# Three gating rows spread over the partitions by a write to memory and a broadcast read, in place of diagonals and a matmul with ones

## The chip, the core and the metric

The kernel runs on one core of a Trainium2 chip. The metric is the device time of one execution in microseconds (us). Shorter is better.

The engines are called as in the profile: PE (matrix products; PEld is its weight load), DVE (vector), ACT (scalar and activation), POOL (GpSimd) and SP (it issues most of the transfers). Each engine works through its own instructions in a fixed order and waits at the first one whose inputs are not ready. Transfers (DMAs) run on 16 DMA engines. SP and POOL each have a queue of them.

## The reference, cut to what matters

Two layers over 512 tokens of width 1024. Each layer has a mixer and an MLP, and each of the four results is multiplied by a gating row (`g1` or `g2`) of 1024 numbers that is the same for all tokens:

```python
c_act = jax.nn.silu(c)
for i in range(DEPTH):
    mod = c_act @ ada_w[i] + ada_b[i]
    sh1, sc1, g1, sh2, sc2, g2 = jnp.split(mod, 6, axis=-1)
    h = modulate(rmsnorm(x, norm_mix_g[i]), sh1, sc1)
    y = pool_mixer(...) if i == 0 else sgu_mixer(...)
    x = x + g1[:, None, :] * y
    h = modulate(rmsnorm(x, norm_mlp_g[i]), sh2, sc2)
    x = x + g2[:, None, :] * sq_relu_mlp(h, mlp_w1[i], mlp_w2[i])
return rmsnorm(x, final_g)
```

The gating row of the first mixer is handled apart and is not touched. The change is in how the other three (layer 0 `g2`, layer 1 `g1`, layer 1 `g2`) get to the place where they are multiplied.

## The kernel before, in words

Tokens lie on the 128 partitions, in four tiles of 128 tokens (`X(t)`, 128x1024). For the products the normed activations lie transposed, features on partitions, in `hb`, as a high and a low part. Each float32 product of weights and activations is three matmuls of such parts (`mm3`, lines 176 to 178). Each weight tile is loaded as `raw` (512 KB, into the three slots of the pool `w4`, helper `raw4`, line 155), and ACT makes the high part `wh` (line 167) and DVE the low part `wl` (line 168). Each of `wh` and `wl` has five slots.

**Modulation.** A column of 128 modulation numbers is the product of 128 columns of `ada_w` and `c_act`. `ada_tile` (line 191) loads a 512 KB tile into a slot of `w4` (line 194) and DVE multiplies and sums it (line 198). Two such sums make two columns of `mods[i]` (line 183). So the 1024 numbers of a gating row stand as 8 columns of 128 partitions, `mods[i][:, c_g(n,0) : c_g(n,0)+8]`.

**Spreading.** The results are multiplied with tokens on partitions, so the row must stand on every partition: the tile `gb` (128x1024). `spread_cols` (line 209) does it: `diagonals` (line 205) makes 8 diagonal matrices `dg` on POOL (line 207), PE multiplies them with a matrix of ones, 512 columns at a time (line 216), and ACT copies the two banks to `gb` (line 217). In two of the three places `dg` takes a slot of `w4`; in the third it is `dgu` in a tile of the second MLP.

**Where `gb` is read.** `gated` (line 959) multiplies each finished piece of a result by it (line 964), adds it to `x`, takes the squares on ACT (line 969), sums them (lines 973, 975), and POOL makes the reciprocal root `rr` (line 223, called by `rms`). `normed` (line 980) scales 2 token tiles by `rr` on ACT (`xs`, line 985), PE turns them (`px`, line 992), and ACT and DVE write `hb`.

**Stages.** (1) Modulation and pool mixer of layer 0, up to about 60 us. (2) `mlp(0)`: hidden units `f` and output products `p` in turn, then the units `q`, which end with `gated`. In it the list `ex` of extra work is popped at an even pace: 8 `ada_tile` of layer 0, then the spread of layer 0's `g2`, then 24 `ada_tile` of layer 1. (3) the gating mixer of layer 1 (SGU): `w_v` products, layer norm (POOL makes `rr` again), `do_u` and `do_mix` (the spread of layer 1's `g1` is the first extra work there, after `u0`), then the product with `w_o`, whose results go through `gated`; the last 8 `ada_tile` (for layer 1's `g2`) run in it. (4) `mlp(1)`: `first1` (line 1130) loads four tiles of `w1f`, and runs them over the first 256 tokens, then over the second 256. `normed(1, 1, 1)` and `spill(1)` (a copy of `x` to memory by POOL, line 1008) stand after the third tile of the first half. Then the units `f` 4 to 7, after the last of which the spread of layer 1's `g2` stands (line 952), then units `s` and `p` up to the `q` units.

**What sets the order.** PE's instructions run in the order in which the code issues them. In the first stage that holds for DVE, ACT and SP as well. Everywhere else a planner orders the instructions of SP, ACT, DVE and POOL when the program is built: at each step it gives an engine the instruction, first in program order, whose inputs and slots it holds to be ready. So a load, or one of the diagonals, can stand far ahead of its place in the code. The lines that the steps below touch are 155, 183, 194, 205 to 217, 223, 761, 964, 992, 1008, 1022 and 1074.

Of the kernel before, what the change touches and what calls it, by code (L numbers as in the profile page):

```python
# [7 lines left out]
F32 = mybir.dt.float32  # L8
F32R = mybir.dt.float32r
AF = mybir.ActivationFunctionType  # L10
ALU = mybir.AluOpType
# [3 lines left out]
P = 128  # L15
D = 1024
S = 512
KD = D // P
# [23 lines left out]
def c_sh(n, k):  # L42
    return 24 * n + 2 * k + 1


def c_g(n, k):
    return 24 * n + 16 + k
# [31 lines left out]
def decoder_kernel(ctx: ExitStack, tc: tile.TileContext, xtok, vecs, rows, fgrow, ada0, adag, ada1, pool_w, w1s, w1, w1f, w1b, w2, w2e, w_v, w_u, w_o, wsT, lnp, bs, out):  # L79
    nc = tc.nc  # L80
    V, A, G, T = nc.vector, nc.scalar, nc.gpsimd, nc.tensor
# [3 lines left out]
    w4 = ctx.enter_context(tc.tile_pool(name="w4", bufs=3))  # L85
# [20 lines left out]
    def bank(name, pool=None):  # L106
        pool = pool or ps
        return pool.tile([P, S], F32, name=name, tag="mm" if pool is ps else "xz")
# [4 lines left out]
    ones = cp.tile([P, P], F32, name="ones")  # L113
# [3 lines left out]
    ident = cp.tile([P, P], F32, name="ident")  # L117
    G.memset(ident, 0.0)
    G.affine_select(out=ident, in_=ident, compare_op=ALU.not_equal, fill=1.0, base=0, pattern=[[-1, P]], channel_multiplier=1)
    mods = [cp.tile([P, 48], F32, name=f"mods{i}") for i in range(2)]  # L120
# [16 lines left out]
    gb = big.tile([P, D], F32, name="gb")  # L137

    def X(t):
        return x_[t // 2][:, t % 2]  # L140

    def H(k, c):

        return h_[0][:, 0, k, c], h_[0][:, 1, k, c]
# [4 lines left out]
    def mod(i, c):  # L149
        return mods[i][:, c : c + 1]  # L150
# [30 lines left out]
    def finish_mods(i, b, pm):  # L181

        V.tensor_tensor(mods[i][:, 2 * b : 2 * b + 2], pm, vec[:, V_ADAB + 48 * i + 2 * b : V_ADAB + 48 * i + 2 * b + 2], ALU.add)
        n, q = divmod(b, 12)
        if q < 8:
            g0 = (V_MIX, V_MLP)[n] + 8 * i + q
            V.scalar_tensor_tensor(scl[i][n][:, q : q + 1], mod(i, 2 * b), 1.0, vec[:, g0 : g0 + 1], ALU.add, ALU.mult)
# [3 lines left out]
    def ada_tile(i, t, src, get):  # L191

        r = get()
        nc.sync.dma_start(r, src)
        b, j = divmod(t, 2)
        if j == 0:
            pmv[i, b] = sm.tile([P, 2], F32, name="pmv", tag="pmv")
        V.scalar_tensor_tensor(r, r, 1.0, cb, ALU.mult, ALU.mult, accum_out=pmv[i, b][:, j : j + 1])  # L198
        if j == 1:
            finish_mods(i, b, pmv.pop((i, b)))  # L200
# [1 line left out]
    def get4():  # L202
        return w4.tile([P, D], F32, name="ada", tag="w4")

    def diagonals(dg, cols):
        for k in range(KD):
            G.tensor_scalar(dg[:, k], ident, cols[:, k : k + 1], None, ALU.mult)

    def spread_cols(cols, dg=None):

        if dg is None:
            dg = w4.tile([P, KD, P], F32, name="dg", tag="w4")
            diagonals(dg, cols)
        for n in range(2):
            po = bank("pb")
            T.matmul(po, ones, dg[:, 4 * n : 4 * n + 4], start=True, stop=True)  # L216
            A.activation(gb[:, S * n : S * n + S], po, AF.Copy)


    def power(v, n):  # L220
# [12 lines left out]
    with (  # L233
# [67 lines left out]
        def rms():  # L301
            v0 = sm.tile([P, NT], F32, name="rv4", tag="rv4")
            V.tensor_scalar(v0, ss, RMS_EPS, None, ALU.add)
            rt.append(power(v0, NT))
# [285 lines left out]
    def parts(o, a):  # L590

        A.activation(o[0], a, AF.Copy)
        V.tensor_tensor(o[1], a, f32(o[0]), ALU.subtract)

    def mlp(i, first, extra, last, ending):
# [3 lines left out]
        with (  # L599
# [56 lines left out]
            def a_sums(step):  # L656


                def a(r, j):
                    return h32[0][:, 4 * j : 4 * j + 4, 256 * r : 256 * r + 256]  # L660

                def operand(pool, tag):
                    t = pool.tile([P, 2, 4, 256], F32R, name="as", tag=tag)
                    return t[:, 0], t[:, 1]

                def minus(o, p, q):
                    V.tensor_tensor(o, p, q, ALU.subtract)

                first, half = slice(0, 256), slice(256, 512)
                if step == 0:  # L670
                    sums_a.update({1: H(slice(0, 4), first), 2: H(slice(4, 8), first), 4: H(slice(4, 8), half)})
                    shift(hx, LINE - GAP)
                    minus(a(1, 1), a(1, 0), a(1, 1))
                    m, o = 5, operand(hx, "hx")
                elif step == 1:
                    minus(a(1, 1), a(1, 1), a(0, 0))
                    m, o = 6, operand(big, "x0")
                elif step == 2:
                    minus(a(0, 0), a(0, 0), a(1, 0))
                    V.tensor_tensor(a(1, 1), a(1, 1), a(0, 1), ALU.add)  # L680
                    m, o = 3, operand(big, "x1")
                else:
                    m, o = 7, H(slice(0, 4), half)
                parts(o, a(0, 0) if m == 7 else a(1, 1))
                sums_a[m] = o
# [214 lines left out]

            gain = mods[i][:, c_g(1, 0) : c_g(1, 0) + KD]
            done = first(put)
            if i:
                dg = su.tile([P, KD, P], F32, name="dgu", tag="u")
                diagonals(dg, gain)
            units = [("f", (0, f)) for f in range(done, 8)]
            for c in range(3):
                if i == 0:
# [17 lines left out]
            def ahead(n):  # L926

                if i == 0:
                    return min(n + 3, len(units))
                m, s = n + 1, items(*units[n])  # L930
                while m < len(units) and m < n + 5:
                    s += items(*units[m])
                    if s > 5 and m > n + 1:
                        break
                    m += 1
                return m
# [4 lines left out]
            for n, (kind, u) in enumerate(units):  # L941
                for m in range(n, ahead(n)):
                    if m not in ready:
                        ready[m] = prep[units[m][0]](units[m][1])
                while at < len(extra) and at < due * (n + 1):
                    extra[at]()
                    at += 1
                run[kind](u, ready[n])
                if i and kind == "f":
                    a_sums(u[1] - 4)  # L950
                    if u == (0, 7):
                        spread_cols(gain, dg)
                if i and u == (3, 1, 4):
                    reload()

# [24 lines left out]
    def normed(hf, i, n):  # L980

        xs = []
        for r in range(2):
            t = w4.tile([P, D], F32, name="xs", tag="w4")
            A.activation(t, X(2 * hf + r), AF.Copy, scale=rms(2 * hf + r))
            xs.append(t)
        c = slice(256 * hf, 256 * hf + 256)
        for k in range(0, KD, 2):
            px = bank("px")
            for q in range(2):  # L990
                for r in range(2):
                    T.transpose(px[:, 256 * q + P * r : 256 * q + P * r + P], xs[r][:, P * (k + q) : P * (k + q) + P], ident)  # L992
            tt = h32[0][:, k : k + 2, c] if h32 else sm.tile([P, 2, 256], F32, name="tt", tag="tmp")
            for q in range(2):
                a, b = scl[i][n][:, k + q : k + q + 1], mod(i, c_sh(n, k + q))
                if q:
                    A.activation(tt[:, q], px[:, 256:512], AF.Identity, bias=b, scale=a)
                else:
                    V.tensor_scalar(tt[:, q], px[:, 0:256], a, b, ALU.mult, ALU.add)
            parts(H(slice(k, k + 2), c), tt)  # L1000


    h32, xd = [], []
    dram = ctx.enter_context(tc.tile_pool(name="dram", bufs=1, space=bass.MemoryType.DRAM))

    def spill(h):
        xd.append(dram.tile([P, 2, D], F32, name=f"xd{h}"))
# [2 lines left out]
    def reload():  # L1010
        for h in range(2):
            x_[h] = big.tile([P, 2, D], F32, name=f"x{h}", tag=f"x{h}")
            G.dma_start(x_[h], xd[h])
        load_fg()
# [4 lines left out]
        return SWEEP  # L1019

    ex = [lambda q=q: ada_tile(0, 40 + q, ada1[q], get4) for q in range(8)]
    ex += [lambda: spread_cols(mods[0][:, c_g(1, 0) : c_g(1, 0) + KD])]
    ex += [lambda q=q: ada_tile(1, q, ada1[8 + q], get4) for q in range(24)]
    mlp(0, first0, ex, gated, lambda: normed(0, 1, 0))


# [6 lines left out]
    with (  # L1033
# [37 lines left out]
                V.tensor_tensor(v, v, lnt[:, n].rearrange("p (a b) -> p a b", a=2), op)  # L1071

        u, gt, wu = {}, {}, {}
        ex = [lambda: spread_cols(mods[1][:, c_g(0, 0) : c_g(0, 0) + KD])]
        ex += [lambda q=q: ada_tile(1, q, ada1[8 + q], get4) for q in range(24, 40)]

        def do_u(n):
# [75 lines left out]
    def last1(t, c0, n, src, y):  # L1153
# [13 lines left out]
        else:  # L1167
# [5 lines left out]
            nc.sync.dma_start(out[t, :, 1], X(t)[:, S:D])  # L1173

    mlp(1, first1, [], last1, lambda: None)


# [77 lines left out]
```

## Time and profile before

| | |
|---|---|
| median of 3 runs | 873.24 us (872.81 to 873.34) |
| the profiled execution | 873.16 us, of which the profile's span is 871.5 us |
| PE busy | 861.0 us (99%) |
| DVE busy | 670.1 us (77%) |
| ACT busy | 451.3 us (52%) |
| POOL busy | 66.9 us (8%) |
| DMA | 161.80 MB, mean 186 GB/s |
| clock granted to PE | 0.997 |

In the rows of the timeline the columns are start and duration in us, engine, line, operation, tile written and tile read, shapes and count; in brackets stand the idle time before and what ended it. A row with "SPq" or "POOLq" is the issuing of a transfer. In a table of windows each engine has its busy us and its count of instructions, then come PE's clock, the share of time in which the 16 DMA engines were busy, and GB/s.

### The profile page before, as it was taken

Reading aid. Unit: us, or ns where it says so; the run is one execution under the profiler, and the core shown is the slowest. Engines: PE = TensorE matmul, PEld = TensorE weight load, DVE = VectorE, ACT = ScalarE, POOL = GpSimd, SP = SyncE. Lnnn points to the kernel's source line nnn. Section 1 sums busy time; section 2 is a strip of 40 time slices with the busy share of each in tenths; the row PEclk is TensorE's granted clock in tenths of the full one; section 3 lists DMA queues with packets and bytes.
Section 4 is the critical chain, followed back from the end, with each engine's and each line's share of the span. In section 5 each row is a group of like instructions: output and inputs, shape, how many; then the busy total and the mean of one; then the engine's idle time right before and its main releaser. Section 6 shows DMA issues by size and latency. Waiting matters only on the chain.

```text
span 871.5 us, 11804 instructions
## 1 busy us (share of the span) xinstructions
PE 861.0 (99%) x4580; PEld 741.6 (85%) x4580; DVE 670.1 (77%) x881; ACT 451.3 (52%) x653; POOL 66.9 (8%) x87
## 2 busy tenths in 40 slices
PE   9999999999999999999999999999999999999996
PEld 7878888788888888888878888999999998999885
DVE  6889696779869886657798866667777698679755
ACT  4285755554444445237333326666765576566521
POOL 3000003000000000000410012000101000100001
PEclk9999999999999999999999999999999999999998
DMA  9969853553554341615548525937758587677302
GB/s 350 417 229 311 274 193 137 193 193 121 181 204 169 128 162 51 215 37 205 193 155 288 185 73 222 319 87 179 171 193 178 156 225 224 136 162 261 123 24 97
DMA packets 39517, 161.80 MB, mean 186 GB/s; under 512 B 4387, under 2 KB 4515, under 8 KB 34214
## 3 DMA queue, kind: packets, MB, share of 16 engines
q1 hardware_dynamic: 35282, 137.72, 44.0%
q0 software_dynamic: 4032, 23.07, 13.0%
q8 instruction: 36, 0.59, 0.3%
q10 hardware_dynamic: 148, 0.27, 0.1%
q14 instruction: 19, 0.16, 0.1%
HBM read 156.84 MB, written 4.19 MB: 185 GB/s over the span
## 4 chain that ended last, share of the span: by engine, by line
PE 97%; ACT 2%; DVE 1%; issue 0%; POOLq 0%; POOL 0%; DVEq 0%; ACTq 0%
PE po L176 17%; PE po L178 17%; PE po L177 17%; PE pm L177 12%; PE pm L176 12%; PE pm L178 12%; PE pg L389 1%; PE pq L423 1%; PE po L1097 1%; PE po L437 1%; PE pg L288 1%; ACT sq L273 1%; PE px L992 1%; PE pb L216 1%; PE pc L288 1%; PE po L564 0%
## 5 line engine op out<-in xcount | busy, mean ns | idle before, releaser
L176 PE MATMUL po<-hb,wl 128*128 128x256 f32 (+1 forms) x624 | 209.5, 336 | 1.3 <-DVE wl L168 1.3
L178 PE MATMUL po<-hb,wh 128*128 128x256 f32 (+1 forms) x624 | 207.9, 333 | 0.0
L177 PE MATMUL po<-hb,wh 128*128 128x256 f32 (+1 forms) x624 | 207.8, 333 | 0.0
L168 DVE TENSOR_TENSOR wl<-raw,wh 128x1024 fp32r<-128x1024 f32 x107 | 130.9, 1224 | 45.6 <-ACT wh L167 45.3
L167 ACT ACTIVATE wh<-raw 128x1024 fp32r<-128x1024 f32 x107 | 112.7, 1057 | 63.1 <-PE pm L178 31.8
L176 PE MATMUL pm<-wh,ol 128*128 128x512 f32 x336 | 130.8, 389 | 0.0
L178 PE MATMUL pm<-wh,oh 128*128 128x512 f32 x336 | 130.8, 389 | 0.0
L177 PE MATMUL pm<-wl,oh 128*128 128x512 f32 x336 | 130.8, 389 | 0.0
L176 PEld LDWEIGHTS po<-hb,wl 128*128 128x128 f32 x624 | 117.2, 188 | 14.6 <-DVE wl L168 1.7
L177 PEld LDWEIGHTS po<-hb,wh 128*128 128x128 f32 x624 | 117.2, 188 | 12.9 <-issue 0.5
L178 PEld LDWEIGHTS po<-hb,wh 128*128 128x128 f32 x624 | 118.0, 189 | 11.8
L168 DVE TENSOR_TENSOR wl<-b,wh 128x1024 fp32r<-128x1024 f32 x60 | 72.8, 1222 | 26.0 <-ACT wh L167 26.0
L198 DVE SCALAR_TENSOR_TENSOR ada<-ada,cb 128x1024 f32<-128x1024 f32 x56 | 68.4, 1222 | 16.6 <-DMA ada<-in_ada 16.4
L178 PEld LDWEIGHTS pm<-wh,oh 128*128 128x128 f32 x336 | 63.1, 188 | 13.1
L176 PEld LDWEIGHTS pm<-wh,ol 128*128 128x128 f32 x336 | 63.1, 188 | 12.3
L177 PEld LDWEIGHTS pm<-wl,oh 128*128 128x128 f32 x336 | 63.1, 188 | 12.2
L167 ACT ACTIVATE wh<-b 128x1024 fp32r<-128x1024 f32 x60 | 63.4, 1056 | 17.5 <-PE pm L178 9.1
L630 ACT ACTIVATE g<-po 128x512 f32<-128x512 f32 x40 | 23.6, 599 | 75.4 <-PE po L178 73.9
L168 DVE TENSOR_TENSOR wl<-bt,wh 128x1024 fp32r<-128x1024 f32 x24 | 29.1, 1223 | 28.8 <-ACT wh L167 28.8
L969 ACT ACTIVATE tmp<-x 128x512 f32<-128x512 f32 (+1 forms) x25 | 15.3, 612 | 66.0 <-DVE x L965 66.0
L857 DVE TENSOR_TENSOR y<-y,pm 128x512 f32<-128x512 f32 x68 | 43.7, 682 | 1.0 <-PE pm L178 1.0
L177 PE MATMUL po<-as,wh 128*128 128x256 f32 x144 | 40.5, 281 | 0.0
(211 smaller groups left out, 1494.7 us busy)
## 6 DMA issues: line engine op xcount, KB each, us to landing
ada<-in_ada SPq DMA_DIRECT2D x72, 512.0 KB, 3.3
b<-in_w SPq DMA_DIRECT2D x21, 1024.0 KB, 4.9
raw<-in_w SPq DMA_DIRECT2D x25, 512.0 KB, 3.7
raw<-in_w1b SPq DMA_DIRECT2D x24, 512.0 KB, 4.7
bt<-in_w POOLq DMA_DIRECT2D x9, 1024.0 KB, 8.0
raw<-in_w2e SPq DMA_DIRECT2D x16, 512.0 KB, 3.2
raw<-in_w1b POOLq DMA_DIRECT2D x12, 512.0 KB, 5.3
wh<-in_ada SPq DMA_DIRECT2D x9, 512.0 KB, 9.6
```

The lines of the kernel that those rows point to most:

```text
L167: A.activation(h, r, AF.Copy)
L168: V.tensor_tensor(l, r, f32(h), ALU.subtract)
L176: T.matmul(o, wl, mh, start=first, stop=False, **kw)
L177: T.matmul(o, wh, ml, start=False, stop=False, **kw)
L178: T.matmul(o, wh, mh, start=False, stop=last, **kw)
L198: V.scalar_tensor_tensor(r, r, 1.0, cb, ALU.mult, ALU.mult, accum_out=pmv[i, b][:, j : j + 1])
L216: T.matmul(po, ones, dg[:, 4 * n : 4 * n + 4], start=True, stop=True)
L273: A.activation(j, X(t)[:, c], AF.Square, scale=D**-0.5, accum_out=out)
L288: T.matmul(o[:, 0:n], ones, what[:, 0:n], start=True, stop=True)
L630: A.activation(t, po, AF.Relu)
L857: V.tensor_tensor(yt, yt, banks[hf], ALU.subtract if minus else ALU.add)
L969: A.activation(tmp, xt, AF.Square, scale=D**-0.5, accum_out=s[:, len(cs) : len(cs) + 1])
```

## The change

`spread_cols` no longer uses POOL's diagonals, PE, or ACT. It writes the 8 columns of 128 numbers to a line of 1024 numbers in memory, by a DMA issued on SP, and reads the line back to `gb` with every partition getting the whole of it, by a DMA issued on POOL. `diagonals`, its 24 instructions, the tile `dg`/`dgu`, 6 matmuls (12 records) and 6 copies are gone. The spread of layer 0's `g2` stands after the fourth `ada_tile` of layer 1 in the list `ex`, not right behind the last of layer 0; the list stays 33 long. The pool in memory is opened earlier in the code.

```diff
-    def diagonals(dg, cols):
-        for k in range(KD):
-            G.tensor_scalar(dg[:, k], ident, cols[:, k : k + 1], None, ALU.mult)
-
-    def spread_cols(cols, dg=None):
-
-        if dg is None:
-            dg = w4.tile([P, KD, P], F32, name="dg", tag="w4")
-            diagonals(dg, cols)
-        for n in range(2):
-            po = bank("pb")
-            T.matmul(po, ones, dg[:, 4 * n : 4 * n + 4], start=True, stop=True)
-            A.activation(gb[:, S * n : S * n + S], po, AF.Copy)
+    dram = ctx.enter_context(tc.tile_pool(name="dram", bufs=1, space=bass.MemoryType.DRAM))
+
+    def spread_cols(cols, name):
+
+        line = dram.tile([KD, P], F32, name=name)
+        nc.sync.dma_start(line.rearrange("k p -> p k"), cols)
+        G.dma_start(gb, line.rearrange("(o k) p -> o (k p)", o=1).to_broadcast([P, D]))
...
-            if i:
-                dg = su.tile([P, KD, P], F32, name="dgu", tag="u")
-                diagonals(dg, gain)
...
-                        spread_cols(gain, dg)
+                        spread_cols(gain, "gain1")
...
-    dram = ctx.enter_context(tc.tile_pool(name="dram", bufs=1, space=bass.MemoryType.DRAM))
...
-    ex += [lambda: spread_cols(mods[0][:, c_g(1, 0) : c_g(1, 0) + KD])]
     ex += [lambda q=q: ada_tile(1, q, ada1[8 + q], get4) for q in range(24)]
+    ex.insert(12, lambda: spread_cols(mods[0][:, c_g(1, 0) : c_g(1, 0) + KD], "gain0"))
...
-        ex = [lambda: spread_cols(mods[1][:, c_g(0, 0) : c_g(0, 0) + KD])]
+        ex = [lambda: spread_cols(mods[1][:, c_g(0, 0) : c_g(0, 0) + KD], "gainm")]
```

## The prediction, made before the changed kernel was run

> **What bounds the kernel now.** I read the page first (busy times, then the chain of work that ended last), then PE's waits.
>
> ```profile
> span 871.5 us, 11804 instructions
> PE 861.0 (99%) x4580; PEld 741.6 (85%) x4580; DVE 670.1 (77%) x881; ACT 451.3 (52%) x653; POOL 66.9 (8%) x87
> ...
> PE 97%; ACT 2%; DVE 1%; issue 0%; POOLq 0%; POOL 0%; DVEq 0%; ACTq 0%
> ```
>
> ```profile
> PE po L176 <- DVE wl L168: 1.3, 1, 1.3
> PE pc L288 <- DVE edge L255: 1.1, 1, 1.1
> PE px L458 <- ACT xf L462: 0.7, 1, 0.7
> ```
>
> PE is the bound: the chain is 97% PE, and PE's three listed waits on other engines come to 3.1 us in all. So an instruction taken from PE shortens the run by its place in the chain, as long as what replaces it makes no wait that PE sees.
>
> **Removed from PE.** The chain of waits has the three spreads as pieces of their own, with no idle time around them:
>
> ```profile
> 158.05 0.23 PE pm L178
> 158.29 1.72 PE pb L216 x4
> 160.01 0.23 PE po L176
> ...
> 446.48 1.72 PE pb L216 x4
> ...
> 585.66 1.72 PE pb L216 x4
> ```
>
> A group's row gives 592 ns for each of the 12 records, 7.1 us in all, but these overlap; the step from one start to the next is what counts, and in the chain four records take 1.72 us. Three times 1.72 is **5.16 us off PE**. Each spread goes at its own place, and PE's later work moves up by as much.
>
> **Removed elsewhere.** Taken off ACT and POOL are:
>
> ```profile
> L217 ACT ACTIVATE gb<-pb x6: 578/589/597, 159.3 to 588.1; 128x512 f32<-128x512 f32 x6
> ```
>
> ```profile
> L207 POOL TENSOR_SCALAR dg<-ident,mods x16: 597/602/2675, 137.7 to 419.9; 128x128 f32<-128x128 f32 x16
> L207 POOL TENSOR_SCALAR dgu<-ident,mods x8: 595/603/1646, 500.4 to 540.4; 128x128 f32<-128x128 f32 x8
> ```
>
> Six copies of 0.59 us (3.5 us) on an engine that is 52% busy, and 24 small products on one that is 8% busy, are not on the chain: 0. In two places a slot of `w4` is free earlier, so loads can only start sooner: 0 as well, with the 1.3 us wait above as the most that a freer stream could give.
>
> **Added.** Each spread is now a write of 1024 numbers on SP and a 512 KB read on POOL. In the line, two numbers of one partition lie 128 numbers apart, so the write falls into 1024 pieces of 4 bytes, 64 on each of 16 engines if they are shared evenly. The trace of before has nothing like it. Nearest rows:
>
> ```profile
> q1 hardware_dynamic: 35282, 137.72, 44.0%
> ...
> raw<-in_w1b POOLq DMA_DIRECT2D x12, 512.0 KB, 5.3
> ...
> vec<-in_vecs SPq DMA_DIRECT2D x1, 68.0 KB, 1.8
> ```
>
> Lower end: `vec`, 128 rows of 544 bytes, 8 on an engine, landed in 1.8 us. Upper end: on q1 the mean packet (3.9 KB) held its engine for 0.44 x 871.5 x 16 / 35282 = 0.174 us; 64 such are 11.1 us, with the 1.8 us on top 12.9 us. By size a piece is far nearer to `vec`'s rows, but there are eight times as many. I take a third of the upper price, 0.06 us a piece: the 16 engines are held for about 4 us and the write lands after 5.5 us. Issuing on SP: 0.33 us for a load of 128 rows (rows below), so 0.33 to 8 x 0.33 = 2.6 us. The read moves 512 KB and lands in about 5.3 us, by the POOL row of that size.
>
> The Trainium skill, page "DMA: Bandwidth & Descriptors", section "Rules for kernel authors", speaks against this write: a strided last dimension becomes one descriptor for each element, and the rule is to rearrange instead. No row of before has such a transfer, so the trace can't confirm it. The same page's formula ("Anatomy of one DMA") would charge these 4 KB about 2.0 us, an estimate that counts bytes and not pieces; by it the write would hide everywhere and the sum would stay at 868.0.
>
> **Is it hidden at the first place?** The last of the eight columns is done at 137.6 (row below) and SP has nothing to issue from 136.5 to 144.8. `gb` is first read at 356.6.
>
> ```profile
> 137.58 0.16 DVE L183 TENSOR_TENSOR mods<-pmv,vec 128x2 f32<-128x2 f32 x1
> ```
>
> ```profile
> 136.19 0.33 SPq L155 DMA_DIRECT2D raw<-in_w  x1
> 144.83 0.33 SPq L761 DMA_DIRECT2D b<-in_w  x1
> ```
>
> ```profile
> L964 DVE TENSOR_TENSOR tmp<-y,gb x15: 691/692/695, 356.6 to 859.2; 128x512 f32<-128x512 f32 x15
> L964 DVE TENSOR_TENSOR tmp<-po,gb x8: 678/692/694, 503.1 to 539.9; 128x512 f32<-128x512 f32 x8
> ```
>
> Over two hundred us of cover for the row itself. At the upper price the load of 144.83 is 6 us late; loads are made two units ahead there, and a unit is 24 matmuls of 0.23 us (the chain's pieces), 5.5 us, so PE has 11 us: 0.
>
> **The second.** The last column of layer 1's `g1` is ready at 355.6; the read has to wait for the last use of the old row, at 398.4; the new one is first used at 503.1. Behind it on POOL stands the `rr` of the last norm of `mlp(0)`.
>
> ```profile
> 355.48 0.16 DVE L183 TENSOR_TENSOR mods<-pmv,vec 128x2 f32<-128x2 f32 x1
> ...
> 397.70 0.69 DVE L964 TENSOR_TENSOR tmp<-y,gb 128x512 f32<-128x512 f32 x1
> ```
>
> ```profile
> 380.97 0.58 POOL L223 TENSOR_TENSOR rr<-sums,mhalf 128x1 f32<-128x1 f32 x1 [15.83 <-DVE sums L973]
> ...
> 401.47 0.55 POOL L223 TENSOR_TENSOR rr<-sums,mhalf 128x1 f32<-128x1 f32 x1 [7.72 <-DVE sums L973]
> ```
>
> From 398.4 to 401.5 there is room to issue a read of about 0.85 us: 0.
>
> **The third is the tight one.** Its last column is ready at 538.7, where the second MLP starts:
>
> ```profile
> 538.51 0.16 DVE L183 TENSOR_TENSOR mods<-pmv,vec 128x2 f32<-128x2 f32 x1
> 546.53 1.23 DVE L168 TENSOR_TENSOR wl<-raw,wh 128x1024 fp32r<-128x1024 f32 x1 [2.83 <-ACT wh L167]
> ```
>
> ```profile
> 538.85 0.33 SPq L761 DMA_DIRECT2D bt<-in_w  x1
> 540.05 0.33 SPq L155 DMA_DIRECT2D raw<-in_w1f  x1
> ...
> 547.79 0.33 SPq L155 DMA_DIRECT2D raw<-in_w1f  x1
> ```
>
> ```profile
> 542.75 0.62 POOL L1008 DMA_DIRECT2D xd<-x  x1 [1.75 <-DVE x L965]
> 543.80 0.57 POOL L223 TENSOR_TENSOR rr<-sums,mhalf 128x1 f32<-128x1 f32 x1 [0.42 <-DVE sums L973]
> ```
>
> ```profile
> 548.37 1.91 PE L992 MATMUL px<-ident,xs 128*128 128x128 f32 x16
> 550.03 0.37 PE L176 MATMUL po<-hb,wl 128*128 128x256 f32 x1
> ...
> 550.35 0.28 PE L178 MATMUL po<-hb,wh 128*128 128x256 f32 x1
> ...
> 552.74 0.28 PE L178 MATMUL po<-hb,wh 128*128 128x256 f32 x1
> ```
>
> ```profile
> 540.00:555.00 15.00, 14.92 (x131) 14.93 (x132) 9.98 (x16) 8.51 (x14) 2.19 (x4) 1.00 0.97 369
> ```
>
> The write comes before the `bt` load in program order, so SP likely issues it at 538.7, ahead of the fourth `w1f` load. Then three things can be late. (a) That load: PE needs its `wl` at 550.03 and has it at 547.76, 2.3 us of slack; the write's 4 us, less the 1.35 us between 538.7 and 540.05, is 2.65 us. That is 0.4 us too much, unless the load had landed well before ACT took it. (b) `rr` at 543.80: if the planner puts the read ahead of it, POOL stands until the write lands (538.7 + 5.5 = 544.2), issues the read (0.85) and the spill (0.62), and `rr` starts at 545.7, 1.9 us late. `xs`, the fourth `wh` and `wl` follow it with the same 2.3 us of slack: 0. (c) The fifth `w1f` load at 547.79, in a window whose DMA engines are busy 97% of the time: ACT waits for it until 556.42, its `wl` ends at 558.7, and PE needs it after five more runs of 24 matmuls from 550.03 on, at 0.114 us each (the rows of 550.35 and 552.74 are 21 matmuls apart), near 563.7: slack 5 us against 2.65 for the write and 512 KB at 369 GB/s, 1.4 us: 0.
>
> ```profile
> 556.42 1.06 ACT L167 ACTIVATE wh<-raw 128x1024 fp32r<-128x1024 f32 x1 [2.83 <-DMA raw<-in_w1f]
> ```
>
> So I take 0 at the third place, with bounds from -1.3 us (the wait of 1.3 us at 540 us gone with the freer stream) to +8.5 us (the upper price: 11.1 us less 1.35 us is 9.75 us of delay; less 2.3 us of slack that is 7.5 us, and 1 us more for the spill and the read ahead of `rr`).
>
> **The sum** is made against the profiled execution: 871.5 us of span and 1.7 us around it, 873.16 us, 0.08 us below the median. 873.16 - 5.16 = **868.0 us**, 0.6% less.
>
> **Rivals.**
>
> *A short stall at the start of the second MLP.* A piece costs 0.09 to 0.15 us and not 0.06: 64 pieces are 5.8 to 9.6 us, less 1.35 and 2.3, so 2.1 to 6 us. For it: the 97% window. Against it: a piece is a thousandth of the mean packet. It gives 870 to 874 us.
>
> *Slower: the same write ahead of the fourth `w1f`, at the full packet price.* The saving is eaten where 64 pieces hold the engines for 5.16 + 2.3 + 1.35 = 8.8 us, 0.14 us a piece. At 0.174 us the stall is 7.5 to 8.5 us: 875.5 to 876.5 us. The skill's rule against strided elements points this way. Against it: the engines' mean time is for packets of 3.9 KB.
>
> *Slower: the second read in POOL's queue too early.* It must wait for 398.4, and if the planner puts it ahead of the `rr` of 380.97, that `rr` is 18 us late. The read could go at 398.4, and after it (0.85 us), two `rr` (0.6 each) and the scaling on ACT (about 1.1 us, as the `wh` of the same size) PE would turn at 401.6 what it now turns at 388.5: 13 us, 881 us.
>
> ```profile
> 388.53 1.75 PE px L992 x16
> ```
>
> Against it: a planner that issues what it holds ready has no reason to, and its POOL waits in these rows are those of an engine with nothing else to do.
>
> *Faster: the freer `w4` also ends the 1.3 us wait*: 866.7 us.
>
> *The change doesn't do what it says*: the matmuls go but their time stays, since PE would have to wait there for weights. Against it: PE has no listed wait near 158, 446 or 585, and ACT and DVE run ahead of it. It gives 873 us.
>
> **How the numbers follow.** A measurement of this kernel tells about 0.2% (1.75 us) from no change, so faster is below 871.5 and slower above 875.0. Everything hidden, 867 to 869.5 us: 0.52. Freer stream, 866.7: 0.07. Short stall: 0.16, of which 0.06 ends below 871.5 and 0.10 within 0.2%. No saving: 0.02. Slower by the write: 0.16; by POOL's queue: 0.07. So faster 0.65, same 0.12, slower 0.23. The likeliest case gives the time, 868.0, its own range being 867 to 869.5. The range for all runs from 866.7, the best bound, to 876.0, into the slower case; some 0.1 lies above it and 0.05 below.
>
> **What would show it.** Right: no line 216; PE's matmuls follow each other by 0.23 us where the spreads stood; PE busy near 856 us; PE's waits still near 3 us; the write landing in 2 to 6 us. Wrong: a new wait of PE on `wl` or `px` between 535 and 565 us, with the write ahead of `w1f` on SP or the read ahead of `rr` on POOL; an `rr` near 381 that waits for `gb`. The forecast fails if a piece of 4 bytes costs more than about 0.09 us, or if the planner's new order of SP, ACT and DVE opens a wait elsewhere, which no row of before can exclude.

## The result, and the profile after

The changed kernel takes 880.77 us (median of 4 runs, 880.19 to 881.5) where the kernel before, on the same chip, takes 873.29 us (872.81 to 873.37). The ratio is 1.0086, with a 95% interval of 1.0074 to 1.0099: it is slower by 0.9%.

The head of the changed kernel's page, and PE's waits:

```profile
span 878.7 us, 11755 instructions
PE 857.9 (98%) x4568; PEld 740.9 (84%) x4568; DVE 668.9 (76%) x881; ACT 448.1 (51%) x647; POOL 46.3 (5%) x66
...
PE 95%; DMA 2%; ACT 1%; DVE 1%; issue 0%; POOLq 0%; POOL 0%; DVEq 0%; ACTq 0%
```

```profile
PE px L983 <- ACT xs L976: 9.8, 1, 9.8
PE po L176 <- DVE wl L168: 1.2, 1, 1.2
...
PE po L176 <- DVE hb L587: 0.6, 1, 0.6
```

The 12 matmul records are gone and PE's busy time fell. But there is a new wait of 9.8 us at `px`, a small one on `hb`, and DMA now has 2% of the chain. The place of the long wait is the start of the second MLP. First two rows of the kernel before, PE's first matmul of that MLP and ACT's work on its fourth weight tile, then the changed kernel's timeline there (SP's, POOL's, ACT's and PE's rows):

```profile
540.08 0.38 PE L176 MATMUL po<-hb,wl 128*128 128x256 f32 x1 [1.26 <-DVE wl L168]
...
545.46 1.04 ACT L167 ACTIVATE wh<-raw 128x1024 fp32r<-128x1024 f32 x1
```

```profile
535.95 0.38 SPq L210 DMA_DIRECT2D gain<-mods  x1
536.44 0.51 SPq L755 DMA_DIRECT2D bt<-in_w  x1
537.28 0.33 SPq L155 DMA_DIRECT2D raw<-in_w1f  x1
...
548.50 0.58 POOL L211 DMA_DIRECT2D gb<-gain  x1 [16.42 <-DMA gain<-mods]
549.08 0.54 POOL L998 DMA_DIRECT2D xd<-x  x1
549.63 0.56 POOL L217 TENSOR_TENSOR rr<-sums,mhalf 128x1 f32<-128x1 f32 x1
...
553.50 1.06 ACT L167 ACTIVATE wh<-raw 128x1024 fp32r<-128x1024 f32 x1 [12.11 <-DMA raw<-in_w1f]
554.47 1.13 ACT L976 ACTIVATE xs<-x,rr 128x1024 f32<-128x1024 f32 x1
...
537.31 0.39 PE L176 MATMUL po<-hb,wl 128*128 128x256 f32 x1 [1.23 <-DVE wl L168]
...
555.65 3.46 PE L983 MATMUL px<-ident,xs 128*128 128x128 f32 x15 [9.79 <-ACT xs L976]
```

The third write was issued at 535.95, ahead of the fourth `w1f` load. ACT could take the load at 553.5, 16.2 us after its issue; in the kernel before it took it 5.4 us after (540.05 to 545.46). On POOL the read stood for 16.4 us until the write had landed, and the spill and `rr` behind it with it: `rr` ran at 549.6, where 540.08 - 537.31 = 2.77 us ahead of its old time (543.80) would have been 541.0. ACT had its order from the planner: the fourth `wh` first, then `xs`. So the load ends last on the chain; `rr` was late too, and would have been enough for a wait by itself.

What the DMA engines and PE's clock did meanwhile stands in windows of 2 us of the changed kernel (the last three columns are PE's clock, the DMA engines' busy share and GB/s):

```profile
538.00:540.00 2.00, 2.00 (x20) 2.00 (x19) 2.00 (x3) 0.38 (x1) 0.00 (x0) 1.00 2.05 49
540.00:542.00 2.00, 2.00 (x20) 2.00 (x19) 0.85 (x2) 1.40 (x3) 0.00 (x0) 1.00 0.49 29
542.00:544.00 2.00, 2.00 (x20) 2.00 (x19) 0.00 (x0) 0.00 (x0) 0.00 (x0) 1.00 1.35 41
544.00:546.00 2.00, 1.86 (x17) 1.64 (x15) 0.00 (x0) 0.00 (x0) 0.00 (x0) 1.00 0.41 16
...
550.00:552.00 2.00, 0.00 (x0) 0.00 (x0) 0.00 (x0) 0.00 (x0) 0.19 (x1) 0.50 0.99 397
...
556.00:558.00 2.00, 2.00 (x11) 2.00 (x10) 1.09 (x2) 0.56 (x1) 0.00 (x0) 0.50 1.04 438
...
560.00:562.00 2.00, 2.00 (x20) 2.00 (x19) 1.81 (x4) 1.58 (x4) 0.00 (x0) 1.00 1.03 418
```

In the same stage of the kernel before the engines moved 369 GB/s. Here they moved 16 to 49 GB/s from 538 to 546 us while loads of 3.5 MB (`bt`, `w1f`, two `b`) were waiting, and went to about 400 GB/s once the write was through, at 547.9. A packet counts in the window where it starts, so the busy share can pass 1: the 33 packets of the loads that started from 538 to 546 us took 4.2 us each, where those of the kernel before, from 541 to 549, took 0.31. And PE, idle since 545.9, came back at half its clock: `px` took 3.46 us for 15 of its 16 turns where all 16 took 1.91.

**Where 7.2 us of span come from.** Off PE: -5.16. The wait: +9.79. The turns at half clock: 3.46 - 1.91 = +1.55, and some +0.3 for the first matmuls behind them. At the second place: the second MLP begins 2.77 us earlier, not 2 x 1.72 = 3.44, so +0.67. The sum is +7.15.

The prices of the writes and reads in the changed kernel (KB each, median us from issue to landing):

```profile
gb<-gain POOLq DMA_DIRECT2D x2, 512.0 KB, 8.3
...
gb<-gainm POOLq DMA_DIRECT2D x1, 512.0 KB, 4.0
...
gain<-mods SPq DMA_DIRECT2D x2, 4.0 KB, 10.9
...
gainm<-mods SPq DMA_DIRECT2D x1, 4.0 KB, 12.5
```

### The profile page after: what moved, and what is told of

It reads as the page before. It is cut to its first block, busy times and chain, and to the rows that moved or that the text cites. A ratio compares the mean times of both kernels' runs of the same rounds, so it can differ in the third digit from the quotient of the medians.

```text
span 878.7 us, 11755 instructions
## 1 busy us (share of the span) xinstructions
PE 857.9 (98%) x4568; PEld 740.9 (84%) x4568; DVE 668.9 (76%) x881; ACT 448.1 (51%) x647; POOL 46.3 (5%) x66
## 4 chain that ended last, share of the span: by engine, by line
PE 95%; DMA 2%; ACT 1%; DVE 1%; issue 0%; POOLq 0%; POOL 0%; DVEq 0%; ACTq 0%
PE po L176 17%; PE po L178 17%; PE po L177 17%; PE pm L178 12%; PE pm L177 12%; PE pm L176 12%; DMA raw<-in_w1f 2%; PE po L431 2%; PE pg L383 1%; PE pq L417 1%; PE po L1087 1%; PE px L983 1%; PE pg L282 1%; PE pc L282 1%; PE po L558 0%; PE po L561 0%
```

## The experiments

Theory 1: the third write holds back the loads behind it. Theory 2: the third read, waiting on POOL ahead of `rr`, holds back the norm. Theory 3: it is the planner's new order, or the writes at all three places. "Queued behind" is an order given to the planner for one engine, with no wait for the end of the other instruction. Each run's time stands beside the kernel before on the same chip, since chips differ by a microsecond or two. Where there is one run only, no interval is given. In the edits `roots_` and `loads_` list the `rr` and the 512 KB weight loads so far, `W1F` the places of the `w1f` loads among them, and `reads_` the reads; `ins_of` gives the instruction itself.

**The third spread back on PE.**

```diff
+            if i:
+                dg = su.tile([P, KD, P], F32, name="dgu", tag="u")
+                diagonals(dg, gain)
...
-                        spread_cols(gain, "gain1")
+                        spread_pe(dg)
```

> Only the third spread (layer 1 g2) is put back on PE, with its diagonals; the first two stay by way of memory. Theory 1 (the third write holds back the fourth w1f load, which stands behind it in SP's queue) and theory 2 (the third read stands in POOL's queue ahead of rr and waits there for the write) both expect that the 9.8 us wait of PE at px and the slow clock behind it go: 873.2 less two spreads of 1.72 us, plus about 1 us that the second read seems to cost near 405 us, so 870 to 871 us. Theory 3 (the loss is the new order of the planner, or the writes in all three places) expects that most of the 7.5 us stays: 876 us or more.

Measured: 871.51 us against 874.95, ratio 0.9969 (0.9958 to 0.9981). That is 3.4 us less than before, with no wait at `px` in the second MLP. But for a wait of 0.5 us on `hb`, the loss is at the third place. Theory 3 falls: with the first two writes and their order left, the run is faster than the kernel before.

**The third read behind `rr`, the write left where it was.**

```diff
+        with tc.issue_after(ins_of(roots_[-1])) if name == "gain1" else nullcontext():
+            G.dma_start(gb, line.rearrange("(o k) p -> o (k p)", o=1).to_broadcast([P, D]))
```

> The third read is queued on POOL behind the rr of the last norm, so that nothing on POOL waits for the write; the third write stays where it was, ahead of the fourth w1f load on SP. Theory 1 expects px on time, but PE then waits for the wl of the fourth w1f tile, whose load still lands some 16 us after its issue: a wait of 8 to 10 us and 878 to 881 us. Theory 2 expects no wait and 869 to 871 us.

Measured: 885.44 us against 874.95. The timeline (POOL, ACT, PE):

```profile
541.43 0.56 POOL L224 TENSOR_TENSOR rr<-sums,mhalf 128x1 f32<-128x1 f32 x1 [0.48 <-DVE sums L971]
...
558.00 1.06 ACT L173 ACTIVATE wh<-raw 128x1024 fp32r<-128x1024 f32 x1 [14.82 <-DMA raw<-in_w1f]
...
560.37 0.58 PE L182 MATMUL po<-hb,wl 128*128 128x256 f32 x1 [12.38 <-DVE wl L174]
```

`rr` is on time and PE still waits 12.4 us, now on the fourth `wl`, whose load ACT could take 20.2 us after its issue. Theory 1 is enough by itself. Wait and time are above what it expected (8 to 10 us, 878 to 881); no run shows why.

**The write behind the fourth `w1f` load, the read ahead of both `rr` and the spill.** The spread stands in the code of `first1` ahead of `normed(1, 1, 1)`, and that call is queued behind the read.

```diff
+        with tc.issue_after(ins_of(loads_[W1F[3]])) if name == "gain1" else nullcontext():
+            nc.sync.dma_start(line.rearrange("k p -> p k"), cols)
...
+                    spread_cols(mods[1][:, c_g(1, 0) : c_g(1, 0) + KD], "gain1")
+                    with tc.issue_after(ins_of(reads_[-1])):
+                        normed(1, 1, 1)
+                        spill(1)
```

> The third write is queued on SP behind the fourth w1f load, so that this load is no longer behind it; the third read is put on POOL ahead of both rr and the spill of the last norm. Theory 1 expects that the load's time decides: 869 to 872 us. Theory 2 expects that POOL stands until the write has landed, some 12 us after its issue, near 550 us, and that xs, px and the fourth wh follow: a wait of PE of 7 to 10 us at px and 876 to 881 us.

Measured: 883.79 us against 874.95. The timeline (POOL, then ACT):

```profile
553.21 0.58 POOL L218 DMA_DIRECT2D gb<-gain  x1 [26.79 <-DMA gain<-mods]
553.81 1.08 POOL L224 TENSOR_TENSOR rr<-sums,mhalf 128x1 f32<-128x1 f32 x2
...
543.98 1.06 ACT L173 ACTIVATE wh<-raw 128x1024 fp32r<-128x1024 f32 x1 [3.87 <-DMA raw<-in_w1f]
554.42 2.19 ACT L983 ACTIVATE xs<-x,rr 128x1024 f32<-128x1024 f32 x2 [9.38 <-POOL rr L224]
```

The fourth load is there at 544.0, and `xs` waits for POOL; PE waits 9.8 us at `px`. Theory 2 is enough by itself as well. The time is above the expected 876 to 881; the write took some 16 us here and not 12 (issued at 537.4, read at 553.2). In the changed kernel both held, and hid each other: undoing either alone gained nothing in these two runs.

**The write one load later, the read left to the planner** (the first of the two edits above alone; the read then falls behind `rr`).

> The third write is queued on SP just behind the fourth w1f load, one place later than in the changed kernel; the read then falls behind the rr by itself. If what counts is that this one load stands ahead of the write, it lands some 7 us after its issue, as in the run with the read ahead of rr (6.9 us), its wl is at most 1 us late, and the fifth load has 5 us of slack: PE waits 0 to 3 us in all, the run is 2 to 5 us under the kernel before. If the 1024 pieces hold the engines for all loads around them for 12 us, the fifth w1f load, issued some 9 us behind the write, is late by more than its slack: PE waits 3 to 8 us and the run is within 3 us of the kernel before or above it.

Measured: 875.96 us against 874.34. The timeline (SP, ACT, PE):

```profile
537.01 0.44 SPq L217 DMA_DIRECT2D gain<-mods  x1
...
544.86 20.57 SPq L161 DMA_DIRECT2D raw<-in_w1f  x4
...
542.51 1.06 ACT L173 ACTIVATE wh<-raw 128x1024 fp32r<-128x1024 f32 x1 [0.46 <-DMA raw<-in_w1f]
...
562.75 1.06 ACT L173 ACTIVATE wh<-raw 128x1024 fp32r<-128x1024 f32 x1 [12.56 <-DMA raw<-in_w1f]
...
565.21 0.55 PE L182 MATMUL po<-hb,wl 128*128 128x256 f32 x1 [4.73 <-DVE wl L174]
```

The fourth tile is in time, the fifth is not: PE waits 4.7 us on it. Its load, the first of the four of that row, was issued 7.8 us behind the write and took 17.9 us. The difference of 1.6 us between two single runs is too small to go by; the wait is what shows that the write holds back loads issued well behind it.

**The write behind all eight `w1f` loads** (`W1F[7]` in that edit).

> The third write is queued on SP behind the last of the eight w1f loads; its read follows by itself, later than the rr. Theories 1 and 2 both expect no wait of PE at the start of the second MLP: 873.2 - 5.2 + about 1 us for the second read, 868.5 to 870 us. Theory 3 expects 876 us or more.

Measured: 870.17 us against 874.95, ratio 0.9953 (0.9935 to 0.9971). Theories 1 and 2 hold. Two small waits were left, 0.8 us on `hb` near 407 us and 1.3 us on a `wl` at 623 us. ACT still waited 8.9 us for the eighth load, issued 0.4 us *ahead* of the write:

```profile
569.71 1.06 ACT L173 ACTIVATE wh<-raw 128x1024 fp32r<-128x1024 f32 x1 [8.87 <-DMA raw<-in_w1f]
```

**The third write on ACT's queue, the read behind `rr`.**

```diff
-        nc.sync.dma_start(line.rearrange("k p -> p k"), cols)
+        (nc.scalar if name == "gain1" else nc.sync).dma_start(line.rearrange("k p -> p k"), cols)
...
```

> The third write is issued on ACT, so it stands in another queue than the w1f loads; the third read stands behind rr. If the fourth w1f load was late because it stood behind the write in one queue, it now lands within 6 us of its issue, and the run is within 2 us of the one with the third spread on PE (under the kernel before). If the 1024 pieces hold the 16 engines for whoever comes, the load still lands 10 us or more after its issue, PE waits 5 us or more on its wl, and the run is above the kernel before.

Measured: 882.68 us against 873.64. The timeline (ACT's and SP's rows):

```profile
535.62 0.45 ACTq L216 DMA_DIRECT2D gain<-mods  x1
...
536.94 0.33 SPq L161 DMA_DIRECT2D raw<-in_w1f  x1
...
556.52 1.06 ACT L173 ACTIVATE wh<-raw 128x1024 fp32r<-128x1024 f32 x1 [14.17 <-DMA raw<-in_w1f]
```

Of transfers under way only `bt` stands ahead of the load in its own queue, and ACT can take the load 19.6 us after its issue all the same; PE waits 11.7 us on its `wl`. The write holds back the transfers of the other queue, not only those of its own. The Trainium skill states in "DMA: Bandwidth & Descriptors", "Issuing engines are not separate DMA queues", that DMAs of all issuers run on the same 16 engines, and that another issuer saves only issue time. This trace agrees: the load was as late as with the write on SP.

**The second read behind the layer norm's `rr`**, in addition to the write behind all eight loads.

```diff
+        with tc.issue_after(ins_of(roots_[-1])) if name == "gainm" else nullcontext():
+            G.dma_start(gb, line.rearrange("(o k) p -> o (k p)", o=1).to_broadcast([P, D]))
```

> The third write behind the eighth w1f load as in the run that had only that, and the second read queued on POOL behind the rr of the layer norm, some 50 us later. If the second read's 512 KB, issued just ahead of the four w_v loads, makes the wait of PE on hb near 405 us, that wait (0.6 to 0.8 us, with about 0.5 us more around it) goes: 4 to 4.8 us under the kernel before. If the wait comes from ACT's order there, it stays: about 3.5 us under.

Measured: 869.15 us against 873.64, ratio 0.9950 (0.9936 to 0.9964), 4.5 us less. By time alone that can't be told from the run without this edit (4.8 us less); the traces show the difference. In the changed kernel the second place had shown (POOL, then PE):

```profile
396.83 0.59 POOL L211 DMA_DIRECT2D gb<-gainm  x1 [4.96 <-DVE tmp L955]
...
407.08 0.50 PE L176 MATMUL po<-wh,hb 128*128 128x512 f32 x1 [0.56 <-DVE hb L587]
```

With the read 50 us later PE has no wait on `hb` at all, and the `w_v` load issued just behind the read's old place, at 399.5, lands after 3.2 us where it took 4.3 in the changed kernel. Of the eleven traces with the read near 397 us ten have the wait (0.5 to 0.8 us); in the other one (that with pieces of 32 bytes, below) this load landed after 3.1 us. So the 512 KB beside that `w_v` load cost the wait; the wait on a `wl` near 622 us, 1.1 us here, was left.

**Eight rows in place of 1024 pieces.** PE turns the columns, ACT copies them, and the write is 8 rows of 512 bytes, at all three places.

```diff
-        nc.sync.dma_start(line.rearrange("k p -> p k"), cols)
+        pt = bank("pb")
+        T.transpose(pt[0:KD, 0:P], cols, ident)
+        turned_ = sm.tile([P, P], F32, name="gr", tag="gr", bufs=1)
+        A.activation(turned_[0:KD], pt[0:KD, 0:P], AF.Copy)
+        nc.sync.dma_start(line, turned_[0:KD])
```

> All three spreads still go by way of memory, but PE first turns the 128x8 columns to 8 rows of 128 (one small transpose each), ACT copies them, and the write is 8 rows of 512 bytes in place of 1024 pieces of 4. If the number of pieces makes the price of a write, each lands in 2 to 4 us where the others took 10 to 16, no load near it is late, and the transposes cost PE under 0.3 us each: 4.2 to 5.1 us under the kernel before. If a write to memory and the read that waits for it cost what they cost whatever their pieces, the writes land after 10 us or more, and a wait of over 1 us stays near 405 us or in the second MLP: at most 3.5 us under the kernel before.

Measured: 869.25 us against 873.64, ratio 0.9948 (0.9936 to 0.9961), 4.4 us less than before. Rows of the turn, and of the first write and the read that waits for it (duration in ns min/median/max, then the start):

```profile
L211 PE MATMUL pb<-ident,mods x3: 270/271/271, 191.5 to 583.0; 128*8 128x128 f32 x3
```

```profile
L214 SPq DMA_DIRECT2D gain<-gr x1: 296/296/296, 192.5 to 192.5; - x1
L215 POOL DMA_DIRECT2D gb<-gain x1: 724/724/724, 194.0 to 194.0; - x1
```

The read goes out 1.5 us after the write was issued; at the other two places it is 3.4 us (448.39 to 451.76) and 1.7 us (583.94 to 585.69). PE waits for nothing of the three. Its only waits of a kind that the kernel before does not show, 3.1 us on loads of `in_adag`, lie before 30 us, far ahead of the first spread. But the edit does more than cut the pieces: PE runs in the order of the code, so its transposes put the writes elsewhere, the third at 583.9 us and not ahead of the fourth `w1f` load at 536. The time of this run can't tell a cheaper write from one at a quieter place; only the times from write to read can. This kernel and the one just before beat both the kernel before and the changed one; their intervals do not tell them apart.

**What makes the price.** Four runs change the first write and its read only, at their quiet place; what each leaves out of layer 0's `g2` stands in its text. The third write is as in the changed kernel in all of them, so their times stay at 882 us and more. First the changed kernel itself there, 1024 pieces of 4 bytes, 9.8 us to landing and 10.1 us to the read (9.8 to 12.4 us to landing in the eight traces with this write unchanged):

```profile
137.64 0.39 SPq L210 DMA_DIRECT2D gain<-mods  x1
...
147.74 0.72 POOL L211 DMA_DIRECT2D gb<-gain  x1 [92.02 <-DMA gain<-mods]
```

Half the columns:

```diff
+        kd = KD // 2 if name == "gain0" else KD
+        nc.sync.dma_start(line[0:kd].rearrange("k p -> p k"), cols[:, 0:kd])
...
```

> The first write carries only the first four of the eight columns (512 pieces), and two reads of 256 KB put them into both halves of the row, so the second half of layer 0's g2 is a copy of the first. If a write's time goes with its pieces, it lands about 5 to 6 us after its issue, where the 1024 took 9.8 us; if it is a fixed price of such a write, about 10 us again. The third write is as in the changed kernel: 879 to 886 us.

```profile
117.15 0.39 SPq L211 DMA_DIRECT2D gain<-mods  x1
...
127.59 1.29 POOL L213 DMA_DIRECT2D gb<-gain  x2 [71.96 <-DMA gain<-mods]
```

A miss for the price per piece: 512 pieces, 10.4 us from the write's issue to the read's. So three more; in each, as in the changed kernel and the half write, two 512 KB loads are issued up to 2.6 us ahead of the write. The pieces 64 bytes apart:

```diff
+            apart = dram.tile([KD, P, 16], F32, name=name)
+            nc.sync.dma_start(apart[:, :, 0].rearrange("k p -> p k"), cols)
...
```

> In the first write the same 1024 pieces of 4 bytes go to places 64 bytes apart, and only 8 numbers of one column are read back into the row, the rest of which is set to 1.0, so layer 0's g2 is left out. If pieces that fall side by side into one stretch of memory hold each other up, the write lands within 5 us of its issue where the changed kernel's first write took 9.8 us; if each piece has its price wherever it goes, 9 to 13 us. The third write is as in the changed kernel: 879 to 886 us, in this and the next two runs.

```profile
138.29 0.39 SPq L211 DMA_DIRECT2D gain<-mods  x1
...
143.10 1.09 POOL L213 DMA_DIRECT2D gb<-gain  x1 [87.90 <-DMA gain<-mods]
```

4.8 us from the write's issue to the read's, at 882.0 us in all. Pieces of 32 bytes, each partition's eight numbers side by side:

```diff
+            line = dram.tile([P, KD], F32, name=name)
+            nc.sync.dma_start(line, cols)
...
```

> In the first write each partition's eight numbers go side by side, 128 pieces of 32 bytes, so layer 0's g2 is read back in another order. If the price is that of a piece, an eighth of the pieces lands 3 to 5 us after its issue, most of it the two loads ahead; if it is that many small pieces go into the same 4 KB at all, 9 us or more.

```profile
137.69 0.38 SPq L211 DMA_DIRECT2D gain<-mods  x1
...
142.14 0.72 POOL L212 DMA_DIRECT2D gb<-gain  x1 [86.41 <-DMA gain<-mods]
```

4.5 us, at 882.34 us. One column alone, 128 pieces of 4 bytes in one row of 512:

```diff
+            line = dram.tile([1, P], F32, name=name)
+            nc.sync.dma_start(line.rearrange("k p -> p k"), cols[:, KD - 1 : KD])
...
```

> The first write has only the last of the eight columns, 128 pieces of 4 bytes in one row of 512 bytes, and the read puts this row into all eight parts of layer 0's g2. The half write before it took as long as the whole one, so the price did not go with the number of pieces. If the pieces of one row wait for each other and the rows go side by side, it again lands about 9 to 11 us after its issue; if the price is that of a piece, within 5 us.

```profile
138.25 0.38 SPq L211 DMA_DIRECT2D gain<-mods  x1
...
147.47 1.09 POOL L212 DMA_DIRECT2D gb<-gain  x1 [92.13 <-DMA gain<-mods]
```

9.2 us for an eighth of the pieces. (The run took 891.14 us, outside its expected band: its read, in 1024 pieces of 512 bytes, took 19 us, and PE waited 6.1 us on a `wl` at 172 us.) So neither the number of pieces nor their being small makes the price, but small pieces that lie close together in memory: 128 of them side by side cost as much as eight such rows at once, and the same 1024 laid 64 bytes apart cost half the time, most of it that of the loads ahead.

The traces also keep the time of each single packet. The pieces of 4 bytes are recorded at 9 ns and less, and they do not go out slowly. In the changed kernel's first write the last of them starts 3.9 us after the issue and 6.2 us before the read; at the third place 1.6 us after the issue and 10.4 us before the landing. With half the columns and with one column 7.5 and 6.3 us pass between the last piece and the read, with the pieces 64 bytes apart and those of 32 bytes 1.0 and 0.8 us. So the time passes after the pieces have gone out, and only where pieces of 4 bytes lie side by side. What happens in it no run shows, nor whether those of 32 bytes are cheap for their size or because fewer of them share a stretch of memory.

## Why the prediction was wrong

*What bounds the kernel, and the 5.16 us.* Right. Set beside the kernel before, PE's matmuls in the changed kernel gain 1.7 to 1.8 us at each of the three places. The versions without a long wait came out 4.4 to 4.8 us faster.

*The price of the write.* This is the step that failed: "I take a third of the upper price, 0.06 us a piece ... lands after 5.5 us". In the changed kernel the writes landed after 9.8, 12.5 and 12.0 us, and at the third place the other transfers nearly stopped for some 8 us. The term was less than half of what was measured, and its mechanism was wrong too. The sum lets each piece hold its engine for a time of its own. The runs have 9 ns for a piece, 0.6 us for 64 of them, and then a wait behind the last piece; half or an eighth of the pieces, side by side, make a wait as long. That the landings come near the upper end, 12.9 us, is therefore luck: it was reached with the packets' price and the count, and neither makes the time. The rule of the Trainium skill against a strided last dimension ("DMA: Bandwidth & Descriptors", "Rules for kernel authors") pointed the right way, though a count of elements, which is how the rule puts it, would have missed the last run. The formula of the Trainium skill's same page ("Anatomy of one DMA"), about 2 us for 4 KB, stands there for transfers issued by GpSimd, and this write was issued on SP: the scatter took five to six times as long as it gives, the eight rows of 512 bytes 1.5 to 3.4 us.

*The first place*: hidden, as predicted. *The second*: the order on POOL was as predicted, but not its price, 0 in the prediction and 0.67 us here: I looked at POOL and not at the loads which the read's 512 KB would slow. With the read later, the wait on `hb` was gone.

*The third place.* Its places were read rightly: the write ahead of the fourth `w1f`, the read ahead of the spill and `rr`, little slack in both. The sizes follow from the price: the load some 11 us late (16.2 us after its issue and not 5.4) where 2.65 was predicted, `rr` 8.6 us late where 1.9 was. The upper bound of 8.5 us was too low. It let the load run as soon as the write was through, but the 1 MB of `bt` was queued ahead of it, and ACT had the load only 5.6 us after the write had landed; PE's wait was 9.8 us. It had no term for PE's clock, which cost nearly 2 us after the wait, and none for the 0.67 us of the second place. With these the time came out at 880.77 us, above the range.

*The rivals.* The slower one, the write at the full packet price ahead of the fourth `w1f`, had the place and the path right and was 4 us too low; a price for each piece, which it rests on, is not what the runs show. The chance it had, 0.16, was too small: its condition, 0.14 us a piece, lay within the bounds of the price, 0 and 0.174, and no row spoke for a third of the upper one. The rival of the read ahead of the `rr` near 381 us did not occur; that its 881 us is the measured time is luck. The wait of 1.3 us at 540 us stayed (1.2 us), so the faster rival did not either.

## What to carry to other kernels

Before a scatter of 4-byte pieces goes to memory, turn it on chip: with a transpose of 0.27 us it takes 1.5 to 3.4 us from the write to the read where the scatter took 10 us and more. The version with it, whose writes also stand at other places, is 0.5% faster than the kernel before, as is the one that moves the scatters away from the loads; the scatter ahead of a load that PE needs made it 0.9% slower. Ask of an added transfer not only when its data is needed, but which loads are in flight in those microseconds, and of a waiting instruction on an engine with little work what stands behind it. Where two causes end within a few microseconds of each other, an experiment that undoes one shows nothing gained; each has to be left standing alone.

## What the runs showed of the hardware

- From a write's issue to the read that waits for it: 128 pieces of 4 bytes side by side 9.2 us, 1024 of them in eight rows 10.1, 1024 of them 64 bytes apart 4.8, 128 of 32 bytes 4.5, eight rows of 512 bytes 1.5 to 3.4. In the first two, 6 us pass after the last piece has gone out. How far apart is enough, and what in the memory's path makes it, stays open: no run tells a stretch of 64 bytes from one of 512.
- Behind such a write the other transfers nearly stopped (16 to 49 GB/s with megabytes queued, in the changed kernel, and 4.2 us for a packet that took 0.31 before). A load of another queue was late with it (19.6 us from its issue), and so was one that was issued 0.4 us ahead of it (13.9 us).
- In the changed kernel PE's granted clock went to 0.50 3.6 us after its last matmul and came back 4.1 us after it had work again. Over all runs there are ten waits of PE of more than 4 us; in these it fell after 2.0 to 4.3 us, came back after 3.1 to 6.4 us of work, and stayed at 0.50 for 6.8, 10.2 or 13.7 us. The Trainium skill, "TensorE: Matmul & The Clock Gate", "What's actually happening", gives an idle window of about 3.4 us for this. The changed kernel's 3.6 us agrees; in five of the ten waits the clock fell sooner, after 2.0 to 2.9 us, so the traces do not bear out that a whole window of idling is needed.
